# Earlier sums of squares, a regrouped query tile and a pair of last tiles on GpSimd in a two-layer trunk

## The chip, the cores and the metric

The kernel runs on one core of one Trainium2 chip. The metric is device microseconds (us) of one launch, the median of several runs. One execution was also recorded by the hardware profiler; that is the trace that is read here.

## What is computed

The reference is a trunk of two layers on 256 tokens of width 1024, everything in float32. Each layer is a gated feed-forward block (hidden width 2816), a mixer, and a second feed-forward block, each followed by a residual and a layer norm. The mixer of layer 0 is a recurrence beside chunked linear attention; that of layer 1 is latent attention, the part that the change touches most:

```
def odd_mixer(u, positions, w_in, q_norm_g, w_q_up, kv_norm_g, w_kv_up, w_out):
    cq, ckv, k_pe = jnp.split(u @ w_in, [MLA_Q_RANK, MLA_Q_RANK + MLA_KV_RANK], axis=-1)   # 256, 128, 64
    q = (rms_norm(cq, q_norm_g) @ w_q_up).reshape(B_, S, MLA_HEADS, MLA_NOPE + MLA_ROPE)   # 8 heads, 128 + 64
    kv = (rms_norm(ckv, kv_norm_g) @ w_kv_up).reshape(B_, S, MLA_HEADS, MLA_NOPE + MLA_V)  # 128 + 128
    ...                                       # rotary embedding of q_pe and k_pe
    o = causal_block_attention(q, k, v)
    return o.reshape(B_, S, MLA_HEADS * MLA_V) @ w_out
```

`rms_norm` divides by the root of the mean of squares: over 128 features for ckv, over 256 (two tiles of 128) for cq.

## The kernel before

Activations lie transposed: 128 features on the partitions, 256 tokens along the row. A weight matrix is a stream of 128 x 128 tiles in the order of use (`PLAN`, line 169). SP loads 16 tiles at a time into `wraw` (`dma_to`, line 337). To keep float32 accuracy on a faster form of matmul every weight slab of 8 tiles is split: ACT copies a rounded first part `whi` (line 365), and DVE subtracts it from the raw tile to give the rest, `wlo` (line 374). `mm3` (line 482) then multiplies three times: first part by first part, first part by rest, rest by first part (lines 489 to 491). `W.next` hands out tiles and asks for conversions four slabs ahead (`AHEAD`, line 317). If `W.behind_act` holds an instruction, each conversion on ACT that is asked for afterwards stands behind it in ACT's queue (line 367).

Instructions are written in program order, and a scheduler then fixes the order on each engine, by priority and a model of the times; `tc.high_priority` moves a block forward, and inside `tc.manual_schedule(engines={PE})` TensorE keeps the written order. An engine executes its own list strictly in that fixed order. PSUM has six slots named `mm` and two named `ax`; a slot goes to a new tile when the last reader of the old one is done.

Between two sub-layers stands a `Boundary` (line 676). `stats` (line 793) sums the last output tiles over the features with TensorE into two `ax` slots (the mean and the mean square), centres eight tiles `y` on DVE by subtracting the mean (line 820: four at once, four later, after the loop of values), and has TensorE begin the next sub-layer's first weights on the uncentred tiles at the same time (`ahead`, line 798). Ahead of the attention these first weights are four groups of eight tiles: ckv, cq0, cq1 and kp. Behind each group two DVE operations (lines 861, 862) make its value, which is kept in `self.values`.

`odd` (line 1349) is the latent attention. `norm` (line 1366) takes the values: for each of them ACT squares it (line 1371) and TensorE sums the square over the partitions against a constant tile (line 1372); ACT and DVE make the inverse root (`rsqrt2`, line 921) and the normed values `nhi` and `nlo` (lines 1377, 1378). It is called for ckv alone and then for cq0 and cq1 together, both at high priority, both written behind all four groups. Then come the key and value tiles of all heads (line 1410 on), and the query tiles (`query`, line 1473), in the order `Q_ORDER`: twelve entries, eight plain ones of 6 matmuls and four rotary ones of 12.

The loop of line 1498 runs over heads 0 to 7 and two rounds more. Round i computes the scores of head i (line 1436, ending in `e`, the softmax weights, on DVE and ACT), transposes those of head i-1 (`weights`, line 1454) and multiplies by the values of head i-2 (`values`, line 1463). Query tiles fill TensorE in between: four before the loop, one before every head's scores and one more behind those of odd heads. In rounds 8 and 9, where no scores are left, `output` (line 1490) fills in with the first output tile's matmuls, k = 0 to 2 and 3 to 5.

At the very end of the kernel `finish` (line 891) makes the last layer norm. The last four tiles are centred by TensorE into PSUM (lines 903, 905). DVE multiplies four pairs of tiles by the inverse root `r` (line 909), ACT scales and shifts tiles 0 to 4 (line 915), DVE tiles 5 to 7 (line 913), and three DMAs write the result: tiles 0 and 1, tiles 2 to 4 (issued by ACT), tiles 5 to 7.

Of the kernel before, what the change touches and what calls it, by code (L numbers as in the profile page):

```python
# [16 lines left out]
AF = mybir.ActivationFunctionType  # L17
# [225 lines left out]
def trunk_kernel(ctx: ExitStack, tc: tile.TileContext, cvec, m0a, m0b, m1x, x47, pos, wst, modw, colsd,  # L243
# [53 lines left out]
    def constant(value, shape, tag):  # L297
        t = T(const, shape, tag=tag)
        pool.memset(t, value)
        return t  # L300

    ones_dm = T(const, [P, P], tag="ones_dm")
    vec.memset(ones_dm, 1.0 / DM)
    ones_p = constant(1.0 / P, [P, P], "ones_p")
    neg_row = constant(-1.0, [1, P], "neg_row")
    ones_r = T(const, [P, P], F32R, tag="ones_r")
    eps_c = constant(EPS, [P, 1], "eps_c")
# [368 lines left out]
    class Boundary:  # L676
        def __init__(self, l, s, weight):
            ta.use("abs_reciprocal_sqrt_and_small")
            self.next_table = "silu_and_others" if s != 0 else \
                "natural_log_exp_and_others" if l % 2 == 0 else "abs_reciprocal_sqrt_and_small"  # L680
            self.l, self.s, self.weight = l, s, weight
            self.values = None
            self.done = set()
            self.parts = []
            self.gate = None

            self.lazy = LAZY.get((l, s), 0)
            self.late = []
            self.y = T(main, [P, KD, SEQ], tag="yy")
            self.acc = T(wk, [P, 2, SEQ], tag="acc", bufs=1)  # L690
            o = (l * 3 + s) * KD
            self.g, self.b = col("ln_g", o, KD), col("ln_b", o, KD)
            self.last = l == DEPTH - 1 and s == 2
            if self.last:
                self.hg = T(wk, [P, KD], tag="ag")
                vec.tensor_scalar(self.hg, self.g, -0.5, None, MULT)
            else:

                self.next = (l, s + 1) if s < 2 else (l + 1, 0)
                self.ya = [flat(q, F32R)[:, :KD * (SEQ + 2)].rearrange("p (k c) -> p k c", k=KD) for q in range(2)]  # L700
            if not self.lazy:
                self.prepare(0)
# [90 lines left out]
        def stats(self, y, ysq):  # L793
# [56 lines left out]
            for m, f in early(*self.next):  # L850
                if f in first:
                    ahead(m, f, range(1, KD))
                else:
                    first[f] = mmps()
                    ahead(m, f, range(KD))
                ps = first[f]
                with tc.high_priority(offset=EOFF):
                    wab = T(wk, [P, 2], tag="wab", bufs=4)
                    act.activation(wab, ps[:, SEQ:SEQ + 2], AF.Copy)
                    t = T(wk, [P, SEQ], tag="early", bufs=4)  # L860
                    vec.scalar_tensor_tensor(t, msb, wab[:, 0:1], ps[:, :SEQ], MULT, SUB)
                    vec.scalar_tensor_tensor(t, t, 0.5, r, MULT, MULT)
                self.values.append((t, wab[:, 1:2]))
            if odd_next:
                for k in range(PRE, KD):
                    center(k)

        def u(self, k):

# [21 lines left out]
        def finish(self, mean, e2, v, msb):  # L891
# [14 lines left out]
            r, _ = rsqrt2(v, SEQ)  # L906
            for k in range(0, KD, 2):
                src = y[:, k:k + 2, :] if k < HK else pairs[k].rearrange("p (k s) -> p k s", k=2)
                vec.tensor_tensor(y[:, k:k + 2, :], src, wide(r, 2), MULT)
            for k in range(KD):  # L910
                kk = slice(k, k + 1)
                if k in LVEC:
# [436 lines left out]
    def odd(l, prev):  # L1349
        with tc.tile_pool(name=nm("odd"), bufs=1) as op_, tc.tile_pool(name=nm("ow"), bufs=2) as ow:  # L1350
            vt = T(op_, [P, 2, MH * MV], tag="ovt")
            kn = flat(0)[:, :MH * SEQ].rearrange("p (h s) -> p h s", h=MH)
            qn = flat(1)[:, :MH * SEQ].rearrange("p (h s) -> p h s", h=MH)
            ones_q = T(op_, [P, P], tag="ones_q")
            pool.memset(ones_q, 1.0 / QR)

            cm = T(op_, [P, SEQ], tag="cm")
            pool.memset(cm, 0.0)
# [4 lines left out]
            vec.tensor_scalar(g2[:, 0:1], col("kv_norm_g", 0), -0.5, None, MULT)  # L1363
            vec.tensor_scalar(g2[:, 1:3], col("q_norm_g", 0, 2), -0.5, None, MULT)

            def norm(ids, ones):
                msp = axps()
                for i in ids:
                    t, b = prev.values[i]
                    sq = T(wk, [P, SEQ], tag="sg")  # L1370
                    act.activation(sq, t, AF.Square, bias=b)
                    pe.matmul(msp[:, :SEQ], ones, sq, start=(i == ids[0]), stop=(i == ids[-1]))
                r, _ = rsqrt2(msp[:, :SEQ], SEQ, ow)
                for i in ids:
                    t, b = prev.values[i]
                    vec.scalar_tensor_tensor(t, t, b, r, ADD, MULT)
                    ta.users.append(act.activation(nhi[:, i, :], t, AF.Identity, scale=g2[:, i:i + 1]))
                    vec.scalar_tensor_tensor(nlo[:, i, :], t, g2[:, i:i + 1], nhi[:, i, :].bitcast(F32), MULT, SUB)

            with tc.high_priority():  # L1380
                norm([0], ones_p)
                norm([1, 2], ones_q)
            ta.use("exp_and_others")

            def rope(out, p0, p1):
# [110 lines left out]

            queries(4)
            for i in range(MH + 2):
                if i < MH:
                    prev.residual([i])  # L1500
                queries(1)
                with tc.manual_schedule(engines={PE}):
                    if i < MH:
                        scores(i)
                        queries(i % 2)
                    if i == MH:
                        output(0, range(0, 3))
                    if i == MH + 1:
                        output(0, range(3, 6))
                    if i >= 2:  # L1510
# [135 lines left out]
```

## Time and profile before

| | us |
|---|---|
| median of 3 runs | 1008.31 (1007.86 to 1008.39) |
| the profiled execution, its own time | 1007.84 |
| its span, first to last instruction | 1006.1 |
| between span and time | 1.74 |

TensorE runs at the full granted clock for nearly the whole span (0.997 in the mean). A busy TensorE is not one at its peak, since a matmul overlaps the one before it: the starts tell more than the busy time. In the rows of a timeline the columns are start, duration, engine, line, operation, output<-inputs with shapes, how many, and in brackets how long the engine was idle before and what ended that.

### The profile page before, as it was taken

The numbers are of one execution on the slowest core, as the hardware profiler recorded it, in microseconds if no ns is written. First come the engines' busy times: TensorE is split into PE (matmuls) and PEld (weight loads), VectorE is DVE, ScalarE is ACT, GpSimd is POOL, SyncE is SP. The second block draws the span as 40 slices with busy tenths as digits, with TensorE's granted clock in tenths as the row PEclk, the third lists the DMA queues.
The fourth block names the chain that finished last, engine by engine and source line by source line (L and its number), as shares of the span: only waits on it lengthen the run. The fifth ranks groups of instructions, "written<-read, shape, count | busy, mean of one in ns | idle before, by whom it ended". The sixth has DMA issues, their size and how long they took to land.

```text
span 1006.1 us, 20567 instructions
## 1 busy us (share of the span) xinstructions
PE 995.9 (99%) x8354; PEld 976.0 (97%) x8354; DVE 878.2 (87%) x1511; ACT 611.7 (61%) x1033; POOL 4.6 (0%) x24
## 2 busy tenths in 40 slices
PE   9999999999999999999999999999999999999997
PEld 8999999998999999999999999999999999999996
DVE  6789999998999899999996999999788799666664
ACT  4656655578886766645554665454568767554542
POOL 0000000000000000000000000000000000000000
PEclk9999999999999999999999999999999999999998
DMA  9998698755467744799975479898743156766501
GB/s 373 421 392 325 252 365 313 296 210 219 158 244 296 297 169 171 298 374 394 342 298 221 171 267 387 326 329 333 281 168 126 50 183 240 283 217 246 190 21 42
DMA packets 36383, 258.79 MB, mean 257 GB/s; under 512 B 4160, under 2 KB 4416, under 8 KB 5312
## 3 DMA queue, kind: packets, MB, share of 16 engines
q1 hardware_dynamic: 36144, 257.09, 67.8%
q8 instruction: 65, 1.06, 0.4%
q10 hardware_dynamic: 144, 0.39, 0.1%
q14 instruction: 30, 0.25, 0.1%
HBM read 256.42 MB, written 1.05 MB: 256 GB/s over the span
## 4 chain that ended last, share of the span: by engine, by line
PE 85%; DVE 8%; ACT 3%; issue 3%; DMA 1%; SPq 0%; DVEq 0%; ACTq 0%
PE mm L491 26%; PE mm L490 25%; PE mm L489 25%; DVE wlo L374 3%; DVE junk L450 2%; DMA wraw<-wst 1%; ACT whi L365 1%; PE mm L1267 1%; PE mm L1268 1%; PE mm L1266 1%; PE ax L490 1%; PE ax L491 1%; PE ax L489 1%; PE ax L1467 0%; PE mm L1441 0%
## 5 line engine op out<-in xcount | busy, mean ns | idle before, releaser
L374 DVE TENSOR_TENSOR wlo<-wraw,whi 128x1024 fp32r<-128x1024 f32 x338 | 408.7, 1217 | 72.6 <-ACT whi L365 71.9
L365 ACT ACTIVATE whi<-wraw 128x1024 fp32r<-128x1024 f32 x338 | 354.0, 1057 | 163.1 <-PE mm L490 117.2
L491 PE MATMUL mm<-uhi,wlo 128*128 128x256 f32 x1624 | 449.1, 277 | 0.2 <-DVE wlo L374 0.2
L489 PE MATMUL mm<-uhi,whi 128*128 128x256 f32 x1624 | 449.3, 277 | 0.0
L490 PE MATMUL mm<-ulo,whi 128*128 128x256 f32 x1624 | 449.1, 277 | 0.0
L491 PEld LDWEIGHTS mm<-uhi,wlo 128*128 128x128 f32 x1624 | 304.6, 188 | 0.7 <-DVE wlo L374 0.4
L489 PEld LDWEIGHTS mm<-uhi,whi 128*128 128x128 f32 x1624 | 304.8, 188 | 0.4 <-ACT uhi L1470 0.2
L490 PEld LDWEIGHTS mm<-ulo,whi 128*128 128x128 f32 x1624 | 304.8, 188 | 0.4
L489 PE MATMUL mm<-hhi,whi 128*128 128x256 f32 x704 | 194.4, 276 | 0.0
L491 PE MATMUL mm<-hhi,wlo 128*128 128x256 f32 x704 | 194.4, 276 | 0.0
L490 PE MATMUL mm<-hlo,whi 128*128 128x256 f32 x704 | 194.4, 276 | 0.0
L450 DVE CUSTOM_DVE_ANT_0 junk<-wraw,cact,cols 128x1024 bf16<-128x1024 f32 x128 | 163.1, 1275 | 4.8 <-DMA wraw<-modw 4.5
L490 PEld LDWEIGHTS mm<-hlo,whi 128*128 128x128 f32 x704 | 132.2, 188 | 0.0
L489 PEld LDWEIGHTS mm<-hhi,whi 128*128 128x128 f32 x704 | 132.2, 188 | 0.0
L491 PEld LDWEIGHTS mm<-hhi,wlo 128*128 128x128 f32 x704 | 132.2, 188 | 0.0
L565 ACT ACTIVATE hhi<-h 128x256 fp32r<-128x256 f32 x88 | 35.8, 413 | 66.4 <-DVE h L947 66.2
L777 ACT ACTIVATE ysq<-yy 128x256 f32<-128x256 f32 x42 | 17.5, 416 | 59.9 <-DVE yy L770 59.6
L947 DVE SCALAR_TENSOR_TENSOR h<-mm,sg 128x256 f32<-128x256 f32 x75 | 30.3, 414 | 6.4 <-PE mm L491 6.4
L566 DVE TENSOR_TENSOR hlo<-h,hhi 128x256 fp32r<-128x256 f32 x88 | 35.6, 414 | 0.1
L770 DVE SCALAR_TENSOR_TENSOR yy<-mm,gate,ax 128x256 f32<-128x256 f32 x48 | 22.9, 478 | 13.8 <-PE mm L491 13.7
L511 ACT ACTIVATE sg<-mm 128x256 f32<-128x256 f32 x75 | 27.4, 367 | 6.1 <-PE mm L491 3.0
L489 PE MATMUL mm<-flat,whi 128*128 128x258 f32 x96 | 28.5, 297 | 0.0
(340 smaller groups left out, 1126.9 us busy)
## 6 DMA issues: line engine op xcount, KB each, us to landing
wraw<-wst SPq DMA_DIRECT2D x170, 1024.0 KB, 5.6
wraw<-modw SPq DMA_DIRECT2D x68, 1024.0 KB, 6.6
hhi<-modw SPq DMA_DIRECT2D x2, 1024.0 KB, 16.1
hlo<-m1x SPq DMA_DIRECT2D x1, 1408.0 KB, 9.7
wraw<-rgw SPq DMA_DIRECT2D x1, 1024.0 KB, 5.5
hlo<-m0b SPq DMA_DIRECT2D x1, 640.0 KB, 4.7
hlo<-m0a SPq DMA_DIRECT2D x1, 512.0 KB, 3.6
hhi<-x SPq DMA_DIRECT2D x1, 512.0 KB, 20.9
```

What stands on the lines that cost most here:

```text
L365: ia = act.activation(hi, raw, AF.Copy)
L374: i = vec.tensor_tensor(lo, raw, hi.bitcast(F32), SUB)
L450: i = vec.tensor_tensor_reduce(junk, t, cact, 1.0, bias, MULT, ADD, self.modcols[(l, v)][:, j:j + 1])
L489: pe.matmul(ps, hi, mh, start=start, stop=False, skip_group_check=shared)
L490: pe.matmul(ps, hi, ml, start=False, stop=False, skip_group_check=shared)
L491: W.last_product = pe.matmul(ps, lo, mh, start=False, stop=stop, skip_group_check=shared)
L511: i = act.activation(out, in_, func, **kw)
L565: act.activation(hi, src, AF.Copy)
L566: return vec.tensor_tensor(lo, src, hi.bitcast(F32), SUB)
L770: i = vec.scalar_tensor_tensor(y, ps, self.gate[:, f:f + 1], ax[:, f, :], MULT, ADD)
L777: act.activation(ysq, y, AF.Square)
L947: vec.scalar_tensor_tensor(h, pu, bu, sg, ADD, MULT)
```

## The change

1. `ones_q`, the constant tile of 1/256, is made once at the start among the constants, on GpSimd, and no longer in `odd`.
2. Ahead of the attention the square and its sum over the partitions are written right behind each of the first three values (a new method `square`, at high priority), in the loop over the groups, and not in `norm`. Each square also becomes `W.behind_act`: conversions of weights asked for after it stand behind it on ACT.
3. `norm` only reads the finished sums.
4. Head 0's round gets a second query tile, behind its scores. All later query tiles move one place forward.
5. The first output tile's k = 0 is computed at the start of round 5, outside the written order, and round 8 has only k = 1 and 2.
6. In `finish` the first pair's product is done as two single tiles, and the second pair's is done by GpSimd and not by DVE.

```
+    ones_q = constant(1.0 / QR, [P, P], "ones_q")
...
+                if odd_next and len(self.values) <= 3:
+                    self.square(len(self.values) - 1)
             if odd_next:
                 for k in range(PRE, KD):
                     center(k)
+        def square(self, i):
+            t, b = self.values[i]
+            if i < 2:
+                self.msp.append(axps()[:, :SEQ])
+            with tc.high_priority():
+                sq = T(wk, [P, SEQ], tag="sg")
+                W.behind_act = act.activation(sq, t, AF.Square, bias=b)
+                pe.matmul(self.msp[-1], ones_q if i else ones_p, sq, start=i < 2, stop=i != 1)
...
-                vec.tensor_tensor(y[:, k:k + 2, :], src, wide(r, 2), MULT)
+                for q in range(k, k + 2) if k == 0 else [k]:
+                    n = 1 if k == 0 else 2
+                    (pool if k == 2 else vec).tensor_tensor(y[:, q:q + n, :], src[:, q - k:q - k + n, :], wide(r, n), MULT)
...
-            ones_q = T(op_, [P, P], tag="ones_q")
-            pool.memset(ones_q, 1.0 / QR)
...
-            def norm(ids, ones):
-                msp = axps()
-                for i in ids:
-                    t, b = prev.values[i]
-                    sq = T(wk, [P, SEQ], tag="sg")
-                    act.activation(sq, t, AF.Square, bias=b)
-                    pe.matmul(msp[:, :SEQ], ones, sq, start=(i == ids[0]), stop=(i == ids[-1]))
-                r, _ = rsqrt2(msp[:, :SEQ], SEQ, ow)
+            def norm(ids, msp):
+                r, _ = rsqrt2(msp, SEQ, ow)
...
-                norm([0], ones_p)
-                norm([1, 2], ones_q)
+                norm([0], prev.msp[0])
+                norm([1, 2], prev.msp[1])
...
             for i in range(MH + 2):
+                if i == 5:
+                    output(0, range(0, 1))
...
-                        queries(i % 2)
+                        queries(i % 2 or i == 0)
                     if i == MH:
-                        output(0, range(0, 3))
+                        output(0, range(1, 3))
```

## Rows read from the trace of the kernel before

**Rows 1.** The page, part 4: the chain that ended last, by engine.
```profile
PE 85%; DVE 8%; ACT 3%; issue 3%; DMA 1%; SPq 0%; DVEq 0%; ACTq 0%
```

**Rows 2.** By stretch: window, length, PE, PEld, DVE, ACT, POOL (instructions), clock, DMA, GB/s.
```profile
690.00:734.00 44.00, 44.00 (x390) 44.00 (x389) 37.34 (x60) 22.72 (x34) 0.00 (x0) 1.00 0.73 269
```

**Rows 3.** Timeline of PE at the sums of squares: the matmul before, then the sum.
```profile
745.92 0.28 PE L491 MATMUL mm<-flat,wlo 128*128 128x258 f32 x1
746.19 0.70 PE L1372 MATMUL ax<-sg,ones_p 128*128 128x256 f32 x2
...
749.48 0.28 PE L491 MATMUL mm<-flat,wlo 128*128 128x258 f32 x1
749.84 0.67 PE L1372 MATMUL ax<-sg,ones_q 128*128 128x256 f32 x2
...
753.04 0.28 PE L491 MATMUL mm<-nhi,wlo 128*128 128x256 f32 x1
753.38 0.70 PE L1372 MATMUL ax<-sg,ones_q 128*128 128x256 f32 x2
```

**Rows 4.** Timeline of ACT: two weight conversions and the squares behind them.
```profile
744.68 1.06 ACT L365 ACTIVATE whi<-wraw 128x1024 fp32r<-128x1024 f32 x1 [0.42 <-PE mm L490]
745.65 0.49 ACT L1371 ACTIVATE sg<-early,wab 128x256 f32<-128x256 f32 x1
...
748.24 1.06 ACT L365 ACTIVATE whi<-wraw 128x1024 fp32r<-128x1024 f32 x1 [0.39 <-PE mm L490]
749.21 0.49 ACT L1371 ACTIVATE sg<-early,wab 128x256 f32<-128x256 f32 x1
```

**Rows 5.** Timeline of DVE: the first two values finished, and the last centring.
```profile
744.08 0.42 DVE L862 SCALAR_TENSOR_TENSOR early<-early,r 128x256 f32<-128x256 f32 x1
...
748.22 0.41 DVE L862 SCALAR_TENSOR_TENSOR early<-early,r 128x256 f32<-128x256 f32 x1
...
748.89 0.41 DVE L820 TENSOR_TENSOR yy<-yy,ax 128x256 f32<-128x256 f32 x1
```

**Rows 6.** Timeline of PE where the query tiles begin.
```profile
758.50 0.51 PE L489 MATMUL mm<-nhi,whi 128*128 128x256 f32 x3
759.07 0.38 PE L490 MATMUL mm<-nlo,whi 128*128 128x256 f32 x1
```

**Rows 7.** Timeline of PE ahead of the first transposes (head 0).
```profile
768.19 0.28 PE L491 MATMUL mm<-nhi,wlo 128*128 128x256 f32 x1
768.90 0.30 PE L1458 MATMUL mm<-ident,e 128*128 128x128 f32 x1 [0.43 <-DVE e L1450]
```

**Rows 8.** Timeline of ACT in round 8: the copy that head 6's values need.
```profile
788.38 0.48 ACT L1460 ACTIVATE pT<-mm 128x384 f32<-128x384 f32 x1
```

**Rows 9.** Timeline of PE, DVE and ACT in finish, up to its last operations.
```profile
998.20 0.69 DVE L909 TENSOR_TENSOR yy<-yy,r 128x512 f32<-128x512 f32 x1
998.93 2.57 ACT L915 ACTIVATE yy<-yy,cols,ag 128x256 f32<-128x256 f32 x5 [1.69 <-DVE yy L909]
999.14 0.59 PE L905 MATMUL mm<-mean,neg_row 1*128 1x512 f32 x1
1000.01 0.68 DVE L909 TENSOR_TENSOR yy<-mm,r 128x512 f32<-128x512 f32 x1
...
1001.26 0.40 DVE L913 TENSOR_SCALAR yy<-yy,ag,cols 128x256 f32<-128x256 f32 x1
```

**Rows 10.** DMA issues: count, KB, median us from issue to landing (tiles 5 to 7).
```profile
outT<-yy SPq DMA_DIRECT2D x1, 384.0 KB, 3.4
```

**Rows 11.** Groups by line on POOL: shapes, count, busy us, mean ns, idle before.
```profile
L1069 POOL TENSOR_SCALAR_AFFINE_SELECT cmask<-cmask 128x512 int8<-128x512 int8 x1 | 0.6, 634 | 0.0
...
L1359 POOL TENSOR_SCALAR_AFFINE_SELECT cm<-cm 128x128 f32<-128x128 f32 x1 | 0.3, 344 | 0.0
```

**Rows 12.** Timeline of POOL and DVE at the start: the identity and its first reader.
```profile
1.64 0.29 POOL masks.py:199 TENSOR_SCALAR_AFFINE_SELECT ident<-ident 128x128 f32<-128x128 f32 x1
...
2.92 1.29 DVE L544 TENSOR_TENSOR flat<-ident,chi 128x512 fp32r<-128x512 f32 x2
```

More of the change, by code (lines that the diff above doesn't have):

```diff
@@ L684, in __init__ @@
             self.parts = []
+            self.msp = []
             self.gate = None
```

## The prediction

> **What bounds the kernel now.** I read the chain that ended last first: most of it is TensorE [rows 1], so an edit pays only where TensorE stands still or behind its last matmul. The view by stretch gives the pace against which standing still is measured: 390 matmuls in 44.00 us, 0.113 us from start to start of a 256-column matmul when nothing is waited for [rows 2]. Then I went through TensorE's timeline from 737 to 800, where the attention lies, and compared each start with the one before plus 0.113; the busy columns hide these waits, because a matmul's record overlaps the next. Last the timeline of the final 16 us, where no matmul covers anything.
>
> Five waits lie where the change works. Before the three sums of squares: 745.92 + 0.11 = 746.03 against 746.19, so 0.16; 749.59 against 749.84, 0.25; 753.15 against 753.38, 0.23 [rows 3]. Before the first product with the rest of the normed queries: three matmuls from 758.50 end their turn at 758.84, the next starts at 759.07, 0.23 [rows 6]. Before head 0's transposes: 768.30 against 768.90, 0.60, with `e` on DVE named as what ended it [rows 7]. Together 1.47 us. That is all the attention part can win by these edits, 0.15% of the kernel.
>
> **The change, part by part.**
>
> *Squares behind the values.* Nothing is added or removed: three squares on ACT, the sums on TensorE. What moves is the order on ACT. Value 0 is finished at 744.08 + 0.42 = 744.50, but its square starts at 745.65, because a weight conversion of 1.06 was ahead in the queue; value 1 is finished at 748.63 and squared at 749.21, again behind a conversion [rows 4, 5]. So the first square can come 1.15 earlier and the second 0.58 earlier, and the inverse roots, `nhi` and `nlo` with them. The 0.23 at the query tiles [rows 6] should then go: its input needs only to come 0.23 earlier. The three waits of TensorE in front of the sums are less certain. TensorE's order is fixed when the kernel is built, the sum stands at the place where the scheduler's model thought the square ready, and the model's error remains when all moves forward together. Bounds: 0 and 0.64; I take half, 0.3. Sum of this part: 0.55 (0 to 0.87).
>
> What is queued behind a later start: conversions. One asked for in the third group now stands behind the second square. In the times of before that square ends at 749.21 + 0.49 = 749.70, so the conversion that started at 744.68 would start 5.0 later [rows 4]. It was asked for four slabs of 24 matmuls ahead, 4 x 24 x 0.113 = 10.8 us [rows 2], and itself takes 1.06 on ACT and on DVE at most four times the 0.41 of a 256-column subtraction, 1.64 [rows 4, 5]. About 3.1 us of cover are left, so I cost it at nothing; without that cover TensorE would wait for weights. SP's loads follow the conversions that free their slots; a delay of these microseconds lies inside the same lead.
>
> *Another query tile by head 0.* It puts 6 matmuls, 0.68 us, in front of head 0's transposes, whose wait is 0.60 [rows 7]. Nothing is gained in work: the tiles only come one place earlier, and round 5 gets 3 matmuls where it had 6. The wait vanishes if DVE and ACT don't move back too; but the extra tile also has a copy on ACT and the rotary tile behind it three operations of 0.4 on DVE (of the kind of the 0.41 in [rows 5]), and both can come in front of head 0's softmax. Gain between 0 and 0.60. The price is at the other end: round 8 has 3 matmuls fewer, 0.34 us, while ACT's copy for head 6's values still ends at 788.86 [rows 8]; if the scheduler puts matmuls of k = 3 there, nothing is lost. I take 0.35 (between -0.34 and 0.60).
>
> *The end.* DVE's four products follow each other at (1000.01 - 998.20) / 3 = 0.60, ACT's five at 2.57 / 5 = 0.51; ACT is done at 1001.50, DVE at 1001.66, and its DMA lands 3.4 after issue, about 1 us ahead of the span's end [rows 9, 10]. DVE gives up one pair (0.60) and splits one: two singles at no more than 0.41 each [rows 5] in place of 0.60, up to 0.22 more. That would bring its end 0.4 forward, but the last pair reads what TensorE delivers at 999.14 + 0.59 = 999.73 [rows 9]. It started at 1000.01 and can now start at about 999.8. So a wait for TensorE takes the place of the pair, and DVE's end moves 0.2 only, unless tile 5's scaling is put in front of it (then 0.4). ACT starts when the first single is done, 0.28 earlier (0.69 - 0.41), and reaches its third tile at 998.65 + 2 x 0.51 = 999.67. GpSimd has from 998.20 to then, 1.47 us. No two-input operation on GpSimd is in the trace. The nearest rows: 0.63 for a select on 512 narrow elements, 0.344 for one on 128 float32 elements, four times that 1.38 for 512 [rows 11]; a second input can double it to 2.75. I take 1.38, since it is the type at hand, and ACT then doesn't wait. At 2.75 the third tile starts at 1000.97, ACT ends at 1002.5, 0.84 later than DVE's 1001.66. This part: 0.2 faster, from 0.4 faster to 0.85 slower.
>
> [...]
>
> *The start.* One more GpSimd memset, no longer than the 0.29 of the select beside it, lies before the identity, ready at 1.93. DVE first reads it at 2.92 [rows 12]. Hidden; without that cover it is at most 0.3.
>
> **The sum.** 0.55 + 0.35 + 0.2 = 1.1 us. The profiled execution took 1007.84, 0.47 under the median of the runs, so 1006.7 for such an execution and 1007.2 for the median.
>
> **The rivals.**
>
> 1. *DVE and GpSimd exclude each other at the end.* Both want `r` and a tile from SBUF at 998.2. If GpSimd gets in behind the first single (998.6), the second waits until 1000.0, and DVE's rest follows: 0.4 for it, two pairs of 0.60, three scalings of (1001.66 - 1000.69) / 3 = 0.32 [rows 9], done at 1002.6, 0.9 late. If both singles go first (999.0), GpSimd is done at 1000.4, ACT's third starts at 1000.45, and ACT ends at 1002.0, 0.3 late. In the middle 0.6 slower in place of 0.2 faster: 1008.0. For it: both single products read two SBUF tiles at that time. Against it: the last two pairs read PSUM, so it is at most two instructions. [...]
> 2. *All five waits go.* 0.64 + 0.23 + 0.60 and 0.4 at the end, 1.87: 1006.4. Against it: each would have to be filled, and those before the sums come from an order fixed by a model.
> 3. *The waits return elsewhere.* TensorE reaches the next dependency sooner and waits there, and round 8 loses its 0.34: only the end is won, 1008.1.
> 4. *Slower: the second sum waits for a PSUM slot.* The mean and the mean square hold both `ax` slots. The first sum takes that of the mean square; the second needs that of the mean, whose last reader is the eighth centring, ending at 749.30 [rows 5], or the first sum's. In the code before, the sums were asked for behind these centrings; now ahead of them, with the centrings at lower priority. If TensorE has the second sum soon behind the place of the first (746.19), it stands up to 3.1 us; at half of that, 1.55, the first part's 0.55 is lost too, and the time is 1008.31 + 1.55 - 0.55 = 1009.3, up to 1010.9. It decides from a stall of about 1.1 on. Against it: the scheduler's model knows the slots and places the sum by them.
>
> **How the numbers follow.** The forecast, 1007.2, has 0.42; rival 1 (1008.0) 0.25; rival 2 (1006.4) 0.12; rival 3 (1008.1) 0.12; rival 4 (1009.3) 0.09. About 0.2%, 2.0 us, is what a measurement of this kernel can tell from no change. Faster by more is below 1006.3: half of rival 2, since smaller waits may go with it, and the lower tail of the forecast, 0.13. Slower by more is above 1010.3: the upper part of rival 4 and an order on some engine that I don't foresee, 0.05. Within it 0.82. The range runs from rival 2 less the 0.5 by which runs differ (1007.86 to 1008.39) and a little more, 1005.7, over the bounds of the unknown costs (GpSimd at 2.75: 1008.3; round 8 unfilled: 1007.9) into rival 4, 1008.9.
>
> **What would show it.** The waits before the sums: the start of each sum in `square`, against that of the matmul before it plus 0.113. The order on ACT: squares right behind 744.5 and 748.6 or sooner, conversions behind them, and no TensorE wait that names a conversion. The query tile: six matmuls more between head 0's scores and its transposes, and the wait there gone; in round 8, matmuls of k = 3 ahead of head 6's values. The end: GpSimd's product at about 1.4 us and ACT's third tile without idle time before it; a single product on DVE that starts over 1 us late would show rival 1. The second sum waiting for a line-820 reader would show rival 4. The prediction is wrong if TensorE's pace of 0.113 itself changes, or if work outside these stretches is reordered.

## The result, and the profile after

The changed kernel takes 1010.84 us (1010.42 to 1011.24) against 1008.11 (1007.86 to 1008.88) of the kernel before, nine runs of each: a ratio of 1.0026, 95% interval 1.0017 to 1.0036. It is slower by 2.7 us, above the forecast range of 1005.7 to 1008.9; its profiled execution has a span of 1008.7 us against 1006.1.

The page of the changed kernel, part 4, answers [rows 1]:

```profile
PE 86%; DVE 7%; ACT 3%; issue 2%; DMA 1%; DVEq 0%; ACTq 0%
```

and its view by stretch, with the columns of [rows 2]:

```profile
690.00:734.00 44.00, 44.00 (x391) 44.00 (x390) 37.51 (x59) 22.46 (x32) 0.00 (x0) 1.00 0.71 262
```

TensorE's pace is unchanged (391 matmuls in 44.00 us, clock 1.00). The loss has to be standing time at a few places. To find them I cut each trace at three matmuls that every kernel has: the first sum of the layer norm ahead of the attention, the first sum of the layer norm behind it, and the first sum of the last norm. That gives four stages; their lengths in us, worked out from the starts of these matmuls:

```
                     start  attention  feed-forward   end     span
before              737.40      74.47        181.90  12.36   1006.13
after               736.79      76.92        181.99  12.99   1008.70
squares_held        737.55      76.98        181.90  12.33   1008.76
squares_free        737.89      74.38        181.91  12.33   1006.50
queries_only        737.89      74.21        181.87  12.36   1006.33
end_only            738.07      74.50        181.91  13.13   1007.61
hold_first_two      737.41      75.75        181.91  12.37   1007.43
hold_first          737.42      75.71        181.89  12.34   1007.36
hold_second         737.35      75.47        181.93  12.37   1007.12
hold_third          737.63      73.91        181.91  12.76   1006.22
ones_only           737.49      74.44        181.93  12.33   1006.20
queries_no_out      738.26      74.23        181.87  12.32   1006.69
end_order           737.99      74.46        181.86  12.44   1006.75
held_mended_exp     737.53      75.75        181.90  12.37   1007.55
held_mended_queries 737.45      76.18        181.97  12.34   1007.94
third_and_queries   737.47      73.72        181.89  12.36   1005.44
third_queries_exp   737.33      74.44        181.99  12.34   1006.09
```

The first stage varies by up to 0.9 us among executions with no edit in it (737.40 before, 738.26 in queries_no_out), so as a whole it is compared by medians of runs only. The other stages vary less: kernels with nothing changed in the attention have 74.44 to 74.50 us there (before, end_only, end_order, ones_only), and those with the old end 12.32 to 12.37, but for hold_third, whose last DMA takes 3.8 us from issue to landing against 3.4 [rows 10]. The attention of the changed kernel has 2.45 us more, its end 0.63 more. The run held_mended, described below, has no row since its recorded execution (1023.0 us, against a median of 1008.80) had a granted clock of 0.948 in the mean, and for the same reason one execution of ones_only (1070.61 us, clock 0.888) is left out of its ratio.

TensorE's timeline of the changed kernel at the sums of squares, beside [rows 3]:

```profile
744.57 0.28 PE L492 MATMUL mm<-flat,wlo 128*128 128x258 f32 x1
744.81 0.48 PE L880 MATMUL ax<-sg,ones_p 128*128 128x256 f32 x1
...
746.44 0.29 PE L490 MATMUL mm<-flat,whi 128*128 128x258 f32 x1
746.57 0.66 PE L880 MATMUL ax<-sg,ones_q 128*128 128x256 f32 x2
...
751.67 0.28 PE L491 MATMUL mm<-nlo,whi 128*128 128x256 f32 x1
751.79 0.65 PE L880 MATMUL ax<-sg,ones_q 128*128 128x256 f32 x2
```

Of the three waits 0.12 us is left at the first sum, nothing at the others. But further down the same timeline:

```profile
753.33 0.28 PE L492 MATMUL mm<-nhi,wlo 128*128 128x256 f32 x1
754.47 0.70 PE L1413 MATMUL ax<-cs,half 128*128 128x256 f32 x2 [0.87 <-DVE cs L1411]
...
758.92 0.50 PE L490 MATMUL mm<-nhi,whi 128*128 128x256 f32 x2
760.18 0.38 PE L491 MATMUL mm<-nlo,whi 128*128 128x256 f32 x1 [0.76 <-DVE nlo L1387]
...
770.11 0.28 PE L492 MATMUL mm<-nhi,wlo 128*128 128x256 f32 x1
770.53 0.33 PE L1467 MATMUL mm<-ident,e 128*128 128x128 f32 x1
```

754.47 - 753.33 - 0.11 = 1.03 us for `cs`; 760.18 - 758.92 - 0.23 = 1.03 for `nlo`, where it was 0.23 [rows 6]; 0.31 at head 0, where it was 0.60 [rows 7]. For `cs` nothing was waited for in the kernel before; behind a 512-column matmul the next starts 0.23 later:

```profile
756.92 0.39 PE L1420 MATMUL mm<-whi,nlo 128*128 128x512 f32 x1
757.15 0.59 PE L1404 MATMUL ax<-cs,half 128*128 128x256 f32 x2
```

Four more waits stand at later heads, 0.26, 0.41, 0.27 and 0.22 us (the starts at 783.90, 785.99, 790.84 and 792.73), where the kernel before has one of 0.24 (786.57). Adding up every start in the stage that comes over 0.2 us later than the usual distance from such a matmul gives 2.6 us for the kernel before and 5.0 for the changed one: nearly all of the stage's 2.45 is waits.

VectorE's timeline of the changed kernel names what stood ahead of the two late steps:

```profile
752.80 1.22 DVE L375 TENSOR_TENSOR wlo<-wraw,whi 128x1024 fp32r<-128x1024 f32 x1
753.94 0.48 DVE L1411 SCALAR_TENSOR_TENSOR cs<-early,wab,cs 128x256 f32<-128x256 f32 x1
...
758.50 1.23 DVE L375 TENSOR_TENSOR wlo<-wraw,whi 128x1024 fp32r<-128x1024 f32 x1 [0.97 <-ACT whi L366]
759.65 0.87 DVE L1387 SCALAR_TENSOR_TENSOR nlo<-early,g,nhi 128x256 fp32r<-128x256 f32 x2
```

And ACT's timeline shows why these `wlo` come so late:

```profile
744.18 0.17 ACT L861 ACTIVATE wab<-mm 128x2 f32<-128x2 f32 x1 [1.48 <-PE mm L492]
744.25 0.51 ACT L879 ACTIVATE sg<-early,wab 128x256 f32<-128x256 f32 x1
744.66 1.04 ACT L366 ACTIVATE whi<-wraw 128x1024 fp32r<-128x1024 f32 x1
...
751.17 0.51 ACT L879 ACTIVATE sg<-early,wab 128x256 f32<-128x256 f32 x1
751.59 1.04 ACT L366 ACTIVATE whi<-wraw 128x1024 fp32r<-128x1024 f32 x1
...
757.38 1.09 ACT L366 ACTIVATE whi<-wraw 128x1024 fp32r<-128x1024 f32 x1
```

The squares are first, as the change says. ACT stands 1.48 us where a conversion could have run, since none may run ahead of a square [rows 4]. It hardly stands longer in all, though: between 4 and 20 us after the start of the stage 3.4 us, against 3.2 in the kernel before. What changes is when the conversions come. Counted from the start of the stage, the second to the sixth start 2.1, 2.6, 4.0, 1.6 and 1.9 us later than before, and behind the third square two follow closely (751.59, 752.89). The second half of the first of these, 1.22 us on VectorE, lies ahead of `cs`. The next, at 757.38, is ahead of `nhi` (758.33) on ACT, and its half on VectorE ahead of `nlo`.

The end, VectorE's, GpSimd's and ACT's timelines of the changed kernel, beside [rows 9]:

```profile
1000.14 1.83 DVE L926 TENSOR_TENSOR yy<-yy,r 128x256 f32<-128x256 f32 x2
1001.89 1.27 DVE L926 TENSOR_TENSOR yy<-mm,r 128x512 f32<-128x512 f32 x2
1003.09 1.04 DVE L930 TENSOR_SCALAR yy<-yy,ag,cols 128x256 f32<-128x256 f32 x3
...
1000.26 1.43 POOL L926 TENSOR_TENSOR yy<-yy,r 128x512 f32<-128x512 f32 x1 [262.03 <-DVE r L945]
...
1002.01 2.07 ACT L932 ACTIVATE yy<-yy,cols,ag 128x256 f32<-128x256 f32 x4 [0.81 <-DVE yy L926]
```

Two single products of 0.4 each take 1.83 together: the second isn't done until GpSimd's product (1000.26 to 1001.69) is over. ACT stands 0.81 for it. In the kernel before, the first product came 4.43 us and VectorE's last operation 7.89 us after the start of the stage; now 4.43 and 8.42.

### The profile page after: what moved, and what is told of

Same layout as the page of the kernel before. It is cut to its first block, busy times and chain, and to the rows that moved or that the text cites. A ratio compares the mean times of both kernels' runs of the same rounds, so it can differ in the third digit from the quotient of the medians.

```text
span 1008.7 us, 20565 instructions
## 1 busy us (share of the span) xinstructions
PE 996.1 (99%) x8354; PEld 975.8 (97%) x8354; DVE 879.7 (87%) x1511; ACT 611.5 (61%) x1033; POOL 6.1 (1%) x25
## 4 chain that ended last, share of the span: by engine, by line
PE 86%; DVE 7%; ACT 3%; issue 2%; DMA 1%; DVEq 0%; ACTq 0%
PE mm L490 25%; PE mm L492 25%; PE mm L491 25%; DVE wlo L375 3%; PE mm L987 2%; DVE junk L451 1%; PE mm L1284 1%; PE mm L1285 1%; DMA wraw<-modw 1%; PE mm L1283 1%; PE ax L987 1%; ACT whi L366 1%; PE ax L492 1%; PE ax L490 1%; PE ax L491 1%
```

## The experiments

In every comparison the kernel before ran on the same chip, with a median of 1008.51, 1008.44, 1008.42 or 1008.46 us. All intervals are 95%.

### The three parts by themselves

*squares_held* is the first part of the change alone (squares, their sums and the matrix of ones); *squares_free* is the same without the hold:

```
-                W.behind_act = act.activation(sq, t, AF.Square, bias=b)
+                act.activation(sq, t, AF.Square, bias=b)
```

*queries_only* and *end_only* are the hunks at the query tiles and at the end, each alone.

> Parts 1 to 3 alone: squares behind the values, conversions held behind them. The attention stage, from the first sum of the norm ahead of it to the first of the norm behind it, took 74.5 us before and 76.9 after. Theory A, the held conversions do the harm: ACT stands idle while it holds them, then they and DVE's subtractions come in front of the rotary key tile and the normed queries, and TensorE waits 1.03 us twice as in the changed kernel: the stage takes 76.2 or more, the whole 1.7 us or more over before. Rival B, the harm comes with the query tile moved to head 0: the stage takes 74.5 or less here. The end stays at 12.3 us.

> The same without the one assignment that holds the conversions. Theory A: the two waits of 1.03 are gone, and the earlier squares win what the forecast gave them, the stage takes 73.6 to 74.5 and the whole 0 to 0.9 us under before. Rival C, the earlier squares themselves upset the order (they are at high priority, and the second sum's slot now comes ahead of the centrings): the stage stays over 75.5.

> Parts 4 and 5 alone: a query tile more by head 0, the first output matmuls in round 5. The forecast gave 0.35 us, the wait of 0.60 ahead of head 0's transposes gone: stage 74.1. Theory A': TensorE's waits of the head rounds only change places, as in the changed kernel (1.48 us in five waits there, 1.11 in three before): stage 74.5 to 74.9. Rival B: stage over 75.5.

> Part 6 alone. From the first sum of the last norm to the span's end: 12.33 us before, 12.99 after. Theory: the second single product on DVE stands until GpSimd is done, as in the changed kernel, 12.9 to 13.1, and the whole 0.5 to 0.8 us over before; attention stage 74.5. Rival: the end was late through what came before it, 12.1 to 12.4 here.

Measured: squares_held 1010.57 against 1008.51, ratio 1.0021 (1.0013 to 1.0030); squares_free 1007.89, 0.9994 (0.9986 to 1.0003); queries_only 1008.33, 0.9998 (0.9990 to 1.0007); end_only 1009.19, 1.0007 (0.9998 to 1.0016). Of these only the interval of squares_held leaves out 1; that the others differ from the kernel before rests on the stages of their traces. The three parts, 2.06 - 0.18 + 0.68 = 2.56, make up the 2.7 of the whole, though not wait by wait: head 0 waits 1.22 us in squares_held and 0.31 in the changed kernel, and the later heads the other way round (0.24 and 1.16). Nearly all of the loss is the hold: with it the attention has 76.98 us, without it 74.38, as before. Without the hold a square asked for earlier still stands behind the same conversion, ACT's timeline of squares_free:

```profile
745.16 1.06 ACT L366 ACTIVATE whi<-wraw 128x1024 fp32r<-128x1024 f32 x1 [0.41 <-PE mm L491]
746.13 0.49 ACT L879 ACTIVATE sg<-early,wab 128x256 f32<-128x256 f32 x1
```

So moving the squares in the program does nothing for the attention. What is left of squares_free's 0.62 us lies far away, at the start of the kernel (ones_only, below).

### Which of the holds

```
-                W.behind_act = act.activation(sq, t, AF.Square, bias=b)
+                ia = act.activation(sq, t, AF.Square, bias=b)
+                if i < 2:        # hold_first_two; i == 2 in hold_third, i == 0 in hold_first, i == 1 in hold_second
+                    W.behind_act = ia
```

> Parts 1 to 3, but only the first two squares hold conversions back. With all three the attention stage took 76.98 us, with none 74.37. Theory A2: the third square does the harm. Its value is late, since ACT and DVE come to it only at 751, and two conversions wait for it whose slots are free at 748 and 751; they then stand in front of the key tile and the normed queries. Then the two waits of 1.03 are gone here and the first two sums come without a wait: stage 73.7 to 74.4, the whole 0.1 to 0.8 us under before. Rival A1: any held conversion only moves its 2.3 us of ACT and DVE into the fuller stretch behind 752: the stage stays over 75.3.

> The other half: only the third square holds conversions. Theory A2: nearly all of the loss is here, stage 76.0 to 77.2. Rival A1: the loss is shared out by the number of conversions held, one or two of four, stage 75.0 to 75.8.

> The squares right behind the values, only the first of them holding the conversions back. Theory: a held conversion costs where its second half on VectorE comes to lie in front of a step that TensorE awaits; the first square's conversion (744.7 us) has nothing urgent behind it, so by itself it costs nothing and what the two cost together (1.28 us at head 0) belongs to the second: attention 73.9 to 74.5. Rival: the first hold shifts the whole train of conversions by one slot, and head 0's exponential again finds a conversion ahead of it: attention 75.3 to 75.8, with a wait of over 1 us at head 0.

> The squares right behind the values, only the second of them holding the conversions back. Theory: the loss of hold_first_two belongs to this hold: attention 75.3 to 75.8, with a wait of over 1 us for head 0's exponentials, whose scaling on VectorE stands behind a conversion's second half, whole 1008.7 to 1009.3. Rival: it needs both holds, each alone is free or a small gain: attention 73.9 to 74.5, whole 1007.4 to 1008.

Measured: hold_first_two 1009.15 against 1008.44, 1.0007 (0.9998 to 1.0016); hold_third 1007.38, 0.9991 (0.9982 to 1.0000); hold_first 1009.12 against 1008.42, 1.0007 (0.9998 to 1.0016); hold_second 1008.86, 1.0004 (0.9996 to 1.0013). By the attention's length against the 74.38 of squares_free: the first square +1.33, the second +1.09, both +1.37, the third -0.47, all three +2.60. My theories before these runs, that a hold costs by the number of held conversions, or that the third alone does the harm, both fell: the third alone is a gain, and the first and the second together cost no more than one of them. So did the theory that the first has nothing urgent behind it; what was expected of hold_second came.

Most of what a single early hold costs lies some 20 us behind it. ACT's, VectorE's and TensorE's timelines of hold_first at head 0:

```profile
766.26 0.40 ACT L512 ACTIVATE e<-e,nmx 128x128 f32<-128x128 f32 x1 [0.37 <-DVE nmx L1453]
...
766.92 1.05 ACT L366 ACTIVATE whi<-wraw 128x1024 fp32r<-128x1024 f32 x1
767.87 0.50 ACT L512 ACTIVATE e<-e,nmx 128x256 f32<-128x256 f32 x1
...
768.56 0.16 DVE L1457 RECIPROCAL rs<-rs 128x2 f32<-128x2 f32 x1
768.64 1.21 DVE L375 TENSOR_TENSOR wlo<-wraw,whi 128x1024 fp32r<-128x1024 f32 x1
769.76 0.28 DVE L1458 TENSOR_SCALAR e<-e,rs 128x128 f32<-128x128 f32 x1
...
768.68 0.28 PE L492 MATMUL mm<-nhi,wlo 128*128 128x256 f32 x1
770.10 0.33 PE L1466 MATMUL mm<-ident,e 128*128 128x128 f32 x1 [1.15 <-DVE e L1458]
```

A conversion lies between head 0's two exponentials, and its other half between the reciprocal and the scaling; before, ACT's half was ahead of both exponentials (765.92) and VectorE's ahead of the reciprocal (767.07). TensorE waits 770.10 - 768.68 - 0.11 = 1.31 us instead of 0.60; a wait of 0.36 for a copy of values at 760.58 is new too. The hold no longer binds this conversion, since the square was done 21.5 us earlier. Since the queues are fixed ahead of the run, it is the scheduler that comes to another order there when a few conversions 20 us earlier move; what in its model does it isn't shown.

### Putting the order right by hand

These runs tell whether the places in the queues are the cause, or whether held conversions are too late as such. A conversion's half is put behind the step that it stood ahead of:

```
+            queue_behind(W.all_conv[n0 - 1][1], vec.scalar_tensor_tensor(cs, t, b, cs, ADD, MULT))
...
+            queue_behind(W.all_conv[n0 + 1][1], steps["nlo"])
+            for j in range(2):                       # 0: ACT's half, 1: VectorE's
+                queue_behind(W.all_conv[n0 + 4][j], steps[0][j])   # head 0's second exponential, its scaling
```

*held_mended* is squares_held with all three, *held_mended_exp* with the last alone, *held_mended_queries* is held_mended with the query hunk, *third_queries_exp* is third_and_queries (below) with the last alone.

> All three squares hold the conversions as in squares_held, but three orders are set by hand: VectorE's half of one conversion behind cs, that of another behind the last nlo, and one whole conversion (ACT's half behind head 0's second exponential, VectorE's half behind the scaling of head 0's weights). Theory: these three places are where the held conversions cost, 1.04 + (1.03 - 0.23) + (1.22 - 0.56) = 2.50 us against the waits of the kernel without holding; with them mended the attention falls from 76.98 to 74.2 to 74.9 and the whole to 1007.6 to 1008.3. Rival: the sums themselves or the conversions are late as such (ACT stands 1.48 and 1.22 us while nothing may be converted), so that TensorE meets unconverted weights or the next late step instead: attention 75.6 to 76.6, whole 1009.2 to 1010.1.

> Like held_mended, with only the conversion at head 0 put behind its exponentials and scaling; cs and nlo stay behind VectorE's halves. Theory: only head 0's part comes back, 0.66 to 0.9 us, and the waits of 1.04 and 1.03 us for cs and nlo stay: attention 76.1 to 76.3, whole 1009.6 to 1009.9. Rival: the waits at cs and nlo had made head 0 late for itself, so mending it moves its wait to a later head: attention 76.7 to 77.

> third_and_queries with head 0's conversion put behind its second exponential and its scaling. Theory: in third_and_queries no wait over 0.25 us is left ahead of head 0, and what is left is round 8's 0.38 and 0.27; an order at head 0 frees nothing that TensorE awaits: attention 73.5 to 73.9, whole 1007.0 to 1007.4. Rival: the ACT chain of the heads starts earlier, so that the copy of weights in round 8 is earlier too: attention 73.2 to 73.4.

> held_mended with the additional query tile and the moved output tile. Theory: with the three orders mended what the change wanted comes, the sums' waits (0.55 to 0.64) and head 0's (about 0.3) both gone: attention 73.4 to 74.0, whole 1006.8 to 1007.4, as good as third_and_queries. Rival: as for held_mended, the held conversions are late as such: attention 75 to 76, whole 1008.6 to 1009.5.

Measured against 1008.46: held_mended 1008.80, 1.0003 by the medians (the interval, 0.9993 to 1.0037 around 1.0015, takes in the execution of 1023.0 us); held_mended_exp 1009.19, 1.0007 (0.9998 to 1.0015); third_queries_exp 1007.86, 0.9996 (0.9987 to 1.0004); held_mended_queries 1009.63, 1.0012 (1.0003 to 1.0020).

At head 0 the order is the cause. In held_mended_exp TensorE's transposes follow without a wait:

```profile
770.31 0.49 PE L1469 MATMUL mm<-ident,e 128*128 128x128 f32 x3
```

and the attention is 1.23 us shorter than with squares_held, just the 1.22 that the wait was there; this is more than I expected, since the whole wait goes. At `cs` and `nlo` it is different. In held_mended both orders are put right, but the whole is only 0.39 us faster than held_mended_exp (1009.19 - 1008.80), where 1.04 + 0.80 was expected; 1008.80 lies between the theory's 1008.3 and the rival's 1009.2. The trace of held_mended_queries, with the same three orders, shows the first of the waits that took their place, in ACT's and TensorE's timelines:

```profile
752.24 1.04 ACT L367 ACTIVATE whi<-wraw 128x1024 fp32r<-128x1024 f32 x1
...
753.54 1.04 ACT L367 ACTIVATE whi<-wraw 128x1024 fp32r<-128x1024 f32 x1
...
755.56 2.32 ACT L1424 ACTIVATE flat<-mm 128x256 f32<-128x256 f32 x8
...
754.64 0.28 PE L494 MATMUL mm<-nhi,wlo 128*128 128x256 f32 x1
756.00 0.39 PE L492 MATMUL mm<-nhi,whi 128*128 128x256 f32 x1 [1.08 <-ACT flat L1424]
```

The two conversions that waited for the third square come in one lump, and the eight copies of keys out of PSUM stand behind them; TensorE waits 756.00 - 754.64 - 0.11 = 1.25 us for the first. Another wait, of 0.54 us, stands before 761.57, for a copy of values. The trace of held_mended itself has the same two, 1.24 and 0.50, and none at `cs` and `nlo`. So here the rival is right in part: the held conversions are late as such, and if `cs` and `nlo` don't pay for it, the copies behind the conversions do. By the medians the hold costs 2.06 + 0.62 = 2.7 us; the order at head 0 gives 1.3 of it back (among it the 0.56 that was waited there without the hold), those at `cs` and `nlo` 0.4, and 1.0 stays, for which these two waits are more than enough.

Putting an order right isn't safe either. In third_queries_exp head 0's conversion starts at 766.74 and not at 765.46 as in third_and_queries, and this one edit makes waits in the later heads (0.29, 0.42, 0.27 and 0.22 us from 771 to 791, against one of 0.38 in round 8), and the attention 0.72 us longer; neither the theory nor the rival had that. The last three stand in the same places as three of the four waits in the changed kernel and in held_mended_queries, which have the query tile and a late conversion at head 0 too. Of the kernels with only one of the two, queries_only has round 8's alone and squares_held none. So it seems that in the changed kernel the query tile took most of head 0's wait away, and that the late conversion was paid for at later heads instead. Why the queues come out this way isn't shown.

### The query tile

*queries_no_out* leaves `output(0, range(0, 3))` in one piece and only moves the query tile.

> The query tile moved to head 0, but no output matmuls in round 5, so round 8 has its nine. With both moved the stage took 74.21 against 74.47: the wait of 0.60 gone and one of 0.36 new, ahead of head 6's values in round 8. Theory: that 0.36 is the price of the three matmuls taken out of round 8, and it is gone here: stage 73.8 to 73.95, unless round 5, now without fill, waits. Rival: round 8 waits for ACT whatever is in front of it: stage 74.2 or more.

Measured 1008.19 against 1008.44, 0.9997 (0.9988 to 1.0006); attention 74.23, with the output tile moved 74.21. Head 0's wait is gone in both. In queries_only it has come back in part in round 8, TensorE's timeline:

```profile
788.64 0.28 PE L491 MATMUL mm<-uhi,wlo 128*128 128x256 f32 x1
789.11 0.48 PE L1467 MATMUL ax<-pT,ovt 128*128 128x256 f32 x1 [0.19 <-ACT pT L1460]
```

789.11 - 788.64 - 0.11 = 0.36 us for the copy that [rows 8] shows. In queries_no_out three more matmuls are there, and still 789.35 - 789.02 - 0.11 = 0.22 is waited. The moved output tile makes no difference to the stage that these runs show; round 8 waits for ACT whichever way, as the rival had it.

### The end

*end_order* keeps GpSimd's pair, but gives VectorE its five products in an order of their own: a single, a pair out of PSUM, the other single, the last pair.

```
+            for k, n, eng in ((0, 1, vec), (2, 2, pool), (4, 2, vec), (1, 1, vec), (6, 2, vec)):
...
+                    if order is not None:
+                        queue_behind(i, order)
```

> Only the end is changed: GpSimd has its pair, and DVE's order is the first single, the pair of tiles 4 and 5 from PSUM, the second single, the last pair. With the single second it began only when GpSimd was done, and the end took 13.1 against 12.33 us. Theory, DVE and GpSimd exclude each other only where DVE reads two tiles from SBUF: the pair from PSUM starts within 0.4 of the first single and takes 0.68 beside GpSimd, the second single stands until GpSimd's 1.43 are over, and the end takes 12.4 to 12.9. Rival, GpSimd's reads hold up any DVE operation: the pair from PSUM starts only when GpSimd is done, and the end takes 13.0 or more.

Measured 1008.50 against 1008.44, 1.0000 (0.9991 to 1.0009); the end has 12.44 us, against 13.13 in end_only and 12.36 before. VectorE's and GpSimd's timelines:

```profile
998.74 0.42 DVE L910 TENSOR_TENSOR yy<-yy,r 128x256 f32<-128x256 f32 x1
999.08 0.68 DVE L910 TENSOR_TENSOR yy<-mm,r 128x512 f32<-128x512 f32 x1
999.68 0.89 DVE L910 TENSOR_TENSOR yy<-yy,r 128x256 f32<-128x256 f32 x1
...
998.85 1.43 POOL L910 TENSOR_TENSOR yy<-yy,r 128x512 f32<-128x512 f32 x1 [259.41 <-DVE r L933]
```

Beside the same GpSimd product the pair with one input in PSUM takes its usual 0.68, and the single with both inputs in SBUF takes 0.89 instead of 0.42, ending after GpSimd's 1000.28. The order takes the loss away, but no gain comes. VectorE's last operation ends 7.83 us after the start of the stage, 7.89 before; but ACT, which scales tile 1 second, now stands 0.81 us for the late single product, as in the changed kernel, and its last scaling ends at 8.37, where it was 7.73.

### The start, and a version that is faster than both

*ones_only* is the kernel before with nothing but `ones_q` among the constants at the start. *third_and_queries* has the squares with only the third holding, and the query hunk; the end is left as before.

> Only the second matrix of ones is set among the constants at the start and no longer ahead of the attention; no square, query tile or product is moved. Theory: this one line is what makes all kernels that carry it some 0.55 us faster between the 200th and the 400th matmul (32 to 37 us), because the planner then puts one weight conversion on ACT ahead of four copies out of PSUM and VectorE's rest is not late; expected: whole 1007.5 to 1008.1 against 1008.4 of the kernel before, that conversion at about 31.1 us instead of 33.1, attention 74.4 to 74.5. Rival: that gain belongs to the moved squares (two sums' PSUM slots and tiles laid out otherwise), and the memset alone does nothing: 1008.4, conversion at 33.1.

> The squares right behind the values with only the third holding the conversions back, and the additional query tile and output tile as in the change; the end as before. Theory: the two gains lie in different stretches (the sums at 746 to 757 us and head 0's first exponentials), so they add: attention 73.9 - 0.26 = 73.65, whole 1007.4 - 0.3 = about 1007.1, a ratio of 0.9985 to 0.9990, better than both kernels. Rival: with the third held, head 0 comes earlier against its own exponentials, its wait (0.51 with hold_third) is what is left of the chain on ACT and VectorE and a tile in front of it only moves the wait back to round 8: attention 73.9, whole 1007.4.

Measured against 1008.42: ones_only 1007.87, 0.9994 (0.9984 to 1.0003), and third_and_queries 1007.23, 0.9988 (0.9979 to 0.9997).

By matmuls counted from the start, all twelve kernels of the table with the constant at the start have won 0.59 to 0.63 us on the kernel before between the 200th and the 400th, and the four without it nothing (0.03 at most). So the gain is shown, though the interval of ones_only takes in 1. ACT's timeline of the kernel before there, with the wait of TensorE that it leads to:

```profile
30.54 2.07 ACT L986 ACTIVATE flat<-mm 128x512 f32<-128x512 f32 x4 [0.57 <-PE mm L970]
32.46 1.08 ACT L365 ACTIVATE whi<-wraw 128x1024 fp32r<-128x1024 f32 x1
...
34.86 0.39 PE L491 MATMUL mm<-uhi,wlo 128*128 128x256 f32 x1 [0.17 <-DVE wlo L374]
```

and ACT's of ones_only:

```profile
30.53 1.06 ACT L366 ACTIVATE whi<-wraw 128x1024 fp32r<-128x1024 f32 x1
31.50 2.04 ACT L987 ACTIVATE flat<-mm 128x512 f32<-128x512 f32 x4
```

The conversion is now ahead of the four copies, and TensorE no longer waits for its second half (its starts are 0.11 or 0.12 apart from 34.33 to 35.91). One memset of 0.2 us on GpSimd and its tile, moved to the start, have changed the planned order 30 us later. The 0.55 us is in the changed kernel too, and hides a part of its loss: 2.45 + 0.63 + 0.09 - 0.55 = 2.62.

In third_and_queries the gains add as expected: 0.55 at the start, and 74.44 - 73.72 = 0.72 in the attention, where hold_third has 0.53 and queries_only about 0.25. Head 0's transposes follow at the pace:

```profile
768.50 0.28 PE L492 MATMUL mm<-nhi,wlo 128*128 128x256 f32 x1
768.62 0.56 PE L1466 MATMUL mm<-ident,e 128*128 128x128 f32 x3
```

It is 1.2 us faster than the kernel before and 3.9 faster than the changed one (each beside its own runs of before: -1.19 and +2.73).

## Why the prediction was wrong

- *What bounds the kernel.* Right: TensorE's pace did not change, and everything happened at waits. The five waits were read rightly too; that they were "all the attention part can win" bounds the gain, and I used it as if it also said how little could be lost.
- *The squares.* Moving them did nothing for the attention (74.38 in squares_free, 74.44 in ones_only); the gain hangs on the hold, which the forecast took as free. With hold_third it is 0.53 where 0.55 was forecast, but that the sizes agree is partly luck: there the first square is no earlier, the second 0.5 us and the third 2.5, while the forecast reckoned with 1.15 for the first and 0.58 for the second.
- *The conversions held back, costed at nothing.* This is the step that failed. The 3.1 us of cover were reckoned for the consumers of the converted weights, and no wait for weights appeared, so the figure itself held (VectorE's half took 1.22 us, under the 1.64 allowed). What it left out is that a conversion is also 1.04 us of ACT and 1.22 us of VectorE, which have to fit somewhere in two queues with other steps that TensorE awaits. Held, they come up to 4.0 us later, in a lump ahead of `cs` or the copies of keys, and ahead of `nlo`; and the queues behind are planned anew, which put one between head 0's exponentials. Price 2.6 us of attention (76.98 against 74.38) instead of 0.
- *The query tile.* Right by itself: 0.35 forecast, 0.18 by medians and 0.26 by the stage, and head 0's wait went. A wait of 0.36 came in round 8, near the 0.34 put in the bounds, but not for the reason given there: with the three matmuls back (queries_no_out) the stage is no shorter. That the tile, beside a late conversion at head 0, makes waits at later heads was not foreseen.
- *The end.* The forecast (0.2 faster) was wrong, and rival 1 came true with its mechanism and about its size: +0.63 in the stage, +0.68 by medians of end_only, where the rival's middle was +0.6. The GpSimd product came out near its size, 1.43 for 1.38, with some luck, since the 1.38 was scaled up from an operation with one input; the bound of 2.75, an estimate for the second input, was far off. The trace of end_order shows what rival 1 assumed: the product with two SBUF inputs stood until GpSimd was done (0.89 for 0.42), the one with an input in PSUM did not (0.68). I gave rival 1 a chance of 0.25. Nothing in the trace of the kernel before speaks for it or against it, since GpSimd has no two-input operation there; that the two engines don't hold each other up was an assumption of the forecast, which no run had shown.
- *The start.* Costed at nothing, hidden. The memset itself (0.20 us) is hidden: in the changed kernel the identity is ready at 2.08 and VectorE first reads it at 2.99. But its move was worth -0.55 us through the planned order.
- *Rivals 2, 3 and 4.* The second sum didn't wait for its slot (746.57, at the pace). Rival 3 had waits return elsewhere, but at 1008.1 it only let gains vanish; the waits that came were larger than those that went.
- The order that "I don't foresee" was a part of the 0.05 given to slower by more, and is what happened.

## What to carry to other kernels

If an edit makes one engine's work wait for a step, price it not only by who needs the result of the held work, but by what else stands in that work's queues, on every engine that it passes through: how much later it comes, and which steps it will then be ahead of. Where a scheduler fixes the queues by a model, even a small move can change the order tens of microseconds later (here from -0.55 to +1.3 us), so hold as little as gives the gain (one of three squares here) and read the order behind it in the trace. Before a pair of products is given to GpSimd, look whether VectorE reads two SBUF tiles at that time (here such a product took 0.89 or 1.49 us for 0.42).

## What the runs showed of the hardware

A GpSimd product of 128x512 float32 with two SBUF inputs takes 1.43 us (the changed kernel, end_order), against 0.69 for the same product on VectorE [rows 9]. A VectorE product of 128x256 with two SBUF inputs that began while it ran took 1.49 us in the changed kernel and 0.89 in end_order, and ended 0.28 and 0.29 us after GpSimd's. The single before it, begun 0.12 and 0.11 us ahead of GpSimd's, took 0.43 and 0.42. One of 128x512 with an input in PSUM wasn't disturbed (0.68 in end_order).

Two sums of 256 columns in plain float32 that follow each other (line 809, two records of the trace each) take 0.86 us of TensorE in the kernel before, from 993.77 to the next start at 994.63, so 0.43 each; the three products into which such a product is split take 3 x 0.113 = 0.34.
